# A two-layer stick-breaking/RWKV-7 and gMLP trunk on one core: hidden tiles 2048 bytes apart, query/key weights in groups of four, elementwise steps moved from VectorE to ScalarE and GpSimd

## The chip, the cores and the metric

The kernel runs on one core of a Trainium2 chip. The metric is the device time of one execution in microseconds (us), taken as the median of several runs. "Before" is the kernel as it stood, "after" the one with the change.

## The reference, cut to what matters

The input is 256 positions of 2048 float32 values. There are two layers. Layer 0 mixes with 16 stick-breaking attention heads and 16 RWKV-7 heads, layer 1 with a gated unit; each is followed by a squared-ReLU MLP of 8192 hidden columns.

```python
for layer in range(DEPTH):                       # DEPTH = 2
    h = rms_norm(x, norm_mix[layer])
    mix = even_mixer(h, ...) if layer % 2 == 0 else odd_mixer(h, ...)
    x = x + mix
    h = rms_norm(x, norm_ffn[layer])
    x = x + jnp.square(jax.nn.relu(h @ ffn_w1[layer])) @ ffn_w2[layer]
return rms_norm(x, norm_final)

def rwkv7_time_mix(zb, mu, ...):                 # 16 heads of 64, the second half of even_mixer
    zs = zb + (prev(zb) - zb) * mu               # token shift
    r, k, v, xw, xa, xg = split(zs)
    decay, a, g = ...                            # small projections of xw, xa, xg
    kk = k * k_k; kk = kk / norm(kk)             # per head
    k_mod = k * (1.0 + (a - 1.0) * k_a)
    # per step: S = S * w + (S @ -kk) (kk * a)^T + v k_mod^T ; y = S @ r
    y = (y - mean) * rsqrt(var + LNX_EPS) * lnx_w + lnx_b
    bonus = sum(r * k_mod * r_k) * v
    return (y + bonus) * g
```

## The kernel before, in words

Activations lie transposed: a tile of 128 rows holds 128 channels, and its 256 columns are the positions. Every operand of a large product is split into a high part (`hi`, in the type fp32r) and the rest (`lo`), and a product is hi·hi + hi·lo + lo·hi. A hidden tile `h` therefore has 512 columns, 256 high and 256 low, which are 2048 bytes in each partition.

Weights stream from HBM in groups of `KG` = 2 row blocks by up to 512 columns: SP issues the DMAs, ACT casts `raw` to `hi` (L318), DVE subtracts for `lo` (L319), each with three buffers of 4096 bytes. Three loops consume them. `gemm_a` (L379, L382) loads a weight block as the stationary operand and streams an activation tile: 512 columns for `hi`, 256 for `lo`. `gemm_n` (L413 to L415) does the same in three passes of 256 columns. `gemm_b` (L434 to L436) loads the activation tile as the stationary operand and streams 512 weight columns.

Which loop meets which tiles matters below. In layer 0's MLP and in the odd layer's output projection, `gemm_a` streams `h` tiles (4 x 256 pairs of one L379 and one L382 matmul, and 256 such pairs). In layer 1's MLP, `gemm_b` loads `h` tiles for the second product (1440 matmuls of 512 columns, then `gemm_last`). The normalised input `xg` is one buffer whose tiles are 2048 bytes apart.

The pool `hid` hands out 16 buffers again and again. Through `htile` (L216) a tile is allocated with 32 columns too many, so that buffers are 2176 bytes apart, and starts 0 or 16 columns into its buffer. In the program's memory plan buffer number i starts at 66304 + 2176 i bytes: 66304 is a multiple of 256, so even-numbered buffers start at a multiple of 256 bytes and odd-numbered ones 128 bytes past one. The `hi` and `lo` weight buffers start at multiples of 256.

The mixer of layer 0 (`even_mixer`, `rwkv_pair`, `sb_pair`) runs eight pairs of RWKV heads and eight pairs of stick-breaking heads as generators, which are advanced one step after each piece of a weight product (`advance`), so that their small operations lie between the large matmuls. A recording layer then sets the order in which each engine issues. In `rwkv_pair`, in the order of a pair's life: the token shift on POOL and DVE (L821, L825); `kk` and its square (L882, L884); decay factors `E`, `Ei` (L893, L894); `km` (L898, L899); `Z` and `BK` on DVE and POOL (L920 to L923); `rk` for the bonus (L926); the products `pk` (L936); an inverse by levels (`plv`); the scan over four chunks of 64 positions, each `pa` (L1036), `xs` on ACT (L1037), `pa` again (L1043), `SV` on ACT and DVE (L1044, L1045), `pc` (L1049); then the group norm: `var` (L1071), `rsqrt` by three Newton steps on DVE (L262 to L267), `yn` on POOL (L1085) and its transposes `pyt` on PE (L1090).

The two lines that set how long the group norm may take, in calls of the generator:

```python
W_PK, W_RS, W_YN = 2, 8, 4
for _ in range(W_RS): yield      # between rsqrt and yn; W_YN of them between yn and pyt
```

Of the kernel before, what the change touches and what calls it, by code (L numbers as in the profile page):

```python
# [8 lines left out]
F32 = mybir.dt.float32  # L9
F32R = mybir.dt.float32r  # L10
I32 = mybir.dt.int32
AF = mybir.ActivationFunctionType
# [87 lines left out]
class Net:  # L100
# [28 lines left out]
    def load_consts(self):  # L129
        nc, a = self.nc, self.aps  # L130
        self.consts = self.cp.tile([P, NCONST], F32, name="consts")
        o1 = CONST_OFF["ident"][1]
        nc.scalar.dma_start(self.consts[:, 0:o1], a["consts"][:, 0:o1])
        self.cv = {n: self.consts[:, o:o + w] for n, (o, w) in CONST_OFF.items()}
        self.ident = self.cv["ident"]
        self.ones = self.cp.tile([P, P], F32, name="ones")
        nc.gpsimd.memset(self.ones, 1.0)
        self.xT = self.xp.tile([P, KT, T], F32, name="xT")
        prow = self.hp.tile([P, 544], F32, name="prow", tag="h")[:, 0:512]
        nc.gpsimd.memset(prow, 0.0)  # L140
        rows = [prow[:, i * P:(i + 1) * P] for i in range(NPROW)]

        def put(name, ap, n, w=P, q=nc.gpsimd):
            r0 = PARAM_ROWS[name]
            t, r = rows[r0 // P], r0 % P
            q.dma_start(t[r:r + n, 0:w], ap)

        put("norm_mix", a["norm_mix"].rearrange("l (k p) -> (l k) p", p=P), 32, q=nc.scalar)
        x = a["x"][0].rearrange("(b p) d -> p b d", p=P)
        self.xst = self.xp.tile([P, 2, 4, 6], F32, name="xst")  # L150
        self.xrow = []
        for g in range(4):
            self.xrow.append([])
            for b in range(2):
                t = self.hp.tile([P, 544], F32, name="xrow", tag="h")[:, 0:512]
                nc.sync.dma_start(t, x[:, b, g * 512:(g + 1) * 512])
                self.xrow[g].append(t)
        put("norm_ffn", a["norm_ffn"].rearrange("l (k p) -> (l k) p", p=P), 32)
        mu = a["even_mu"]
        put("even_mu", mu[0, 0:3328].rearrange("(k p) -> k p", p=P), 26)  # L160
        r = PARAM_ROWS["even_mu"] + 26
        nc.gpsimd.dma_start(rows[r // P][r % P:r % P + 1, 0:32], mu[0:1, 3328:3360])
        for n in ("w0", "a0", "k_k", "k_a", "lnx_w", "lnx_b"):
            put("even_" + n, a["even_" + n][0].rearrange("(k p) -> k p", p=P), 8)
        put("even_r_k", a["even_r_k"][0].rearrange("(k h) p -> k (h p)", h=2), 8)
        self.par = self.cp.tile([P, NPROWS], F32, name="par")
        self.prow = rows
# [45 lines left out]
        self.rrow = self.xp.tile([P, T], F32, name="rrow")  # L213
        nc.vector.tensor_copy(self.rrow, ps[:, 0:T])

    def htile(self, o):  # L216
        return self.hp.tile([P, 2 * T + 32], F32R, name="h")[:, o:o + 2 * T]

    def new_norm(self, name, layer):
        buf = self.xp.tile([P, KT * 2 * T + 32], F32R, name="xg")  # L220
        o = XG_START[name, layer]
# [35 lines left out]
        nc.vector.tensor_scalar(m, ps[:, 0:2], 1.0 / D, RMS_EPS, op0=ALU.mult, op1=ALU.add)  # L257
        return m

    def rsqrt(self, out, m, q):  # L260
        nc = self.nc
        nc.vector.tensor_scalar(out.bitcast(I32), m.bitcast(I32), 1, None, op0=ALU.logical_shift_right)  # L262
        nc.vector.tensor_scalar(out.bitcast(I32), out.bitcast(I32), -1, 0x5F3759DF, op0=ALU.mult, op1=ALU.add)
        for _ in range(3):
            nc.vector.tensor_tensor(q, out, out, op=ALU.mult)
            nc.vector.scalar_tensor_tensor(q, q, -0.5, m, op0=ALU.mult, op1=ALU.mult)
            nc.vector.scalar_tensor_tensor(out, q, 1.5, out, op0=ALU.add, op1=ALU.mult)  # L267
# [214 lines left out]
    def ffn(self, layer, last):  # L482
# [8 lines left out]
                self.to_tokens()  # L491

        for q in range(4):
            hs = [self.htile(0 if last else 16) for _ in range(KT)]
            for c in range(4):
                def evac(n, ps):
                    a = self.combine(ps)
# [105 lines left out]
    def odd_mixer(self):  # L603
        nc, a = self.nc, self.aps
        w_in = a["odd_w_in"][0]
        with self.tc.tile_pool(name="odd", bufs=1) as op:
# [44 lines left out]
                        yield  # L651
                        nc.vector.tensor_tensor(v, v, lnb[:, s], op=ALU.add)

            ys = [self.htile(0) for _ in range(KT)]
            two = lambda t: t.rearrange("p (b t) -> p b t", b=2)

            def mix(c, us):
# [34 lines left out]
    def even_mixer(self):  # L692
        nc, a = self.nc, self.aps
        w_in = a["even_w_in"][0]
        with self.tc.tile_pool(name="mix", bufs=1) as mp:
# [1 line left out]
            self.new_norm("norm_mix", 0)  # L697
            xg = self.xg
            opnd = lambda k: xg[:, k]
            ys = [self.htile(0) for _ in range(KT)]  # L700
            self.dup = mp.tile([P, 2, T], F32R, name="dup")
            self.fold = [(mp.tile([P, NCH, 2, C], F32, name=f"Td{i}"), mp.tile([P, NCH, 4, C], F32, name=f"RBT{i}"))
                         for i in range(2)]
# [77 lines left out]
            def sb(j):  # L781
# [8 lines left out]
                        nc.vector.tensor_tensor(o, z[:, ::-1], self.rrow[:, ::-1], op=ALU.mult)  # L790
                    qk[n] = o

                self.gemm_n(w_in, 0, [(j * P, P), (SBW + j * P, P)], [P] * 2, opnd, evac_qk)
                self.bg.append((self.sb_pair(j, qk[0], qk[1], vt, ys[j]), 3, j))

            for j in range(NPAIR):
# [25 lines left out]
        return s  # L822

    def shift_mix(self, s, z, mu, rows):
        self.nc.vector.scalar_tensor_tensor(s[0:rows], s[0:rows], mu[0:rows], z[0:rows, 1:T + 1], op0=ALU.mult, op1=ALU.add)  # L825

    def shift(self, z, mu, rows):
        s = self.shift_sub(z, rows)
# [3 lines left out]
    def rwkv_pair(self, j, rkv, y_out):  # L832
# [46 lines left out]
        mix = lambda n, s: self.shift_mix(s, rkv[n], self.pcol("even_mu", n * 8 + j), P)  # L879
        mix(1, k)  # L880
        kk = st("kk")
        nc.vector.tensor_scalar(kk, k, self.pcol("even_k_k", j), None, op0=ALU.mult)  # L882
        kk2 = st("kk2")
        nc.scalar.square(kk2, kk)  # L884
        yield
        cs = st("cs", NCH * W1)
        nc.vector.tensor_tensor_scan(cs, cv["reset"], sig, 0.0, op0=ALU.mult, op1=ALU.add)
# [7 lines left out]
        yield  # L895
        mix(0, r)
        km = st("km")
        nc.vector.tensor_scalar(km, ai, self.hka[:, j:j + 1], self.oka[:, j:j + 1], op0=ALU.mult, op1=ALU.add)  # L898
        nc.vector.tensor_tensor(km, km, k, op=ALU.mult)  # L899
        pb = self.bank("pn2")  # L900
        for c in range(NCH):
# [21 lines left out]
            nc.gpsimd.tensor_tensor(Z[g, h, :, 1 - h], E3[g, :, 1:W1], ch(r)[g], op=ALU.mult)  # L923
            yield
        rk = st("rk")
        nc.vector.scalar_tensor_tensor(rk, r, self.pcol("even_r_k", j), km, op0=ALU.mult, op1=ALU.mult)  # L926
        for _ in range(W_PK):
            yield
        A = self.tmp("A", bufs=2, tag="comb")
# [142 lines left out]
        yield  # L1072
        rs = mt("rs", NCH)
        rq = mt("rsq", NCH)
        self.rsqrt(rs, var, rq)
        for _ in range(W_RS):
            yield
        yn = st("yn")
# [105 lines left out]
```

## Time and profile before

| | before |
|---|---|
| median of 3 runs | 2323.26 us (2320.88 to 2326.68) |
| the profiled execution, own time | 2320.03 us |
| its span | 2318.3 us |
| PE busy | 2271.3 us, 98% |
| DVE busy | 1492.6 us, 64% |
| ACT busy | 1056.0 us, 46% |
| POOL busy | 367.0 us, 16% |
| DMA | 400.98 MB, mean 173 GB/s |
| chain that ended last, by engine | PE 85%, DVE 8%, DMA 2%, ACT 2%, issue 1%, POOL 1% |

The span is the profiled execution from its first to its last instruction; 1.7 us of its time lie around it. PE's row of busy tenths reads 7 in the first of 40 slices, 8 in the last and 9 in between. The mixer of layer 0 fills the first 475 us, its output projection the next 107; the MLP of layer 0 begins at 582 us, the odd layer at 1306, and the MLP of layer 1 at 1590.

### The profile page before, as it was taken

To read this page: it belongs to the slowest core of one execution; us is meant where nothing else is said; L and a number is where in the kernel's file an instruction comes from. 1 tells how busy PE (TensorE), PEld (TensorE's weight loads), DVE (VectorE), ACT (ScalarE), POOL (GpSimd) and SP (SyncE) were. 2 spreads that over 40 slices of the span, in tenths; PEclk is the share of its full clock that TensorE was granted. 3 is DMA by queue.
4 is the path that set the end of the run, shared out by engine and by line. 5 is a ranking of instruction groups with operands and counts; after the bars stand their busy time and mean duration, and the time that the engine had idled before them with its cause. 6 is when DMAs were issued, how large, how long until landed. Compare 5 with 4: busy or idle time off the path is not lost.

```text
span 2318.3 us, 40151 instructions
## 1 busy us (share of the span) xinstructions
PE 2271.3 (98%) x15818; PEld 1988.1 (86%) x15818; DVE 1492.6 (64%) x2324; ACT 1056.0 (46%) x1571; POOL 367.0 (16%) x498
## 2 busy tenths in 40 slices
PE   7999999999999999999999999999999999999998
PEld 7788888889888888888888889988888888888887
DVE  6778888867655565565567758677555654654655
ACT  5435554444444444454444443444444443543443
POOL 2223333324004103103202202022000000000000
PEclk9999999999999999999999999999999999999999
DMA  6434434365665665665665565565656656666664
GB/s 183 140 108 107 128 105 107 103 196 179 206 186 187 191 186 186 191 187 187 189 188 175 185 191 165 172 200 164 198 189 188 188 190 192 187 189 190 189 189 138
DMA packets 276254, 400.98 MB, mean 173 GB/s; under 512 B 15852, under 2 KB 107489, under 8 KB 275681
## 3 DMA queue, kind: packets, MB, share of 16 engines
q1 hardware_dynamic: 273360, 393.03, 55.9%
q10 hardware_dynamic: 2384, 5.33, 0.6%
q8 instruction: 124, 2.03, 0.4%
q14 instruction: 66, 0.53, 0.1%
q0 software_dynamic: 320, 0.06, 0.0%
HBM read 396.26 MB, written 2.10 MB: 172 GB/s over the span
## 4 chain that ended last, share of the span: by engine, by line
PE 85%; DVE 8%; DMA 2%; ACT 2%; issue 1%; POOL 1%; SPq 0%; DVEq 0%; ACTq 0%; POOLq 0%
PE gm L379 13%; PE g L379 12%; PE gl L379 7%; PE gm L382 6%; PE g L382 6%; PE g L413 4%; PE gl L382 4%; PE g L414 4%; PE g L415 4%; PE g L434 3%; PE g L435 3%; PE g L436 3%; DVE lo L319 3%; PE gm L436 2%; PE gm L434 2%; PE gm L435 2%
## 5 line engine op out<-in xcount | busy, mean ns | idle before, releaser
L319 DVE TENSOR_TENSOR lo<-rawd,hi 128x1024 fp32r<-128x1024 f32 x600 | 749.4, 1250 | 625.2 <-ACT hi L318 620.0
L318 ACT CAST hi<-rawd 128x1024 fp32r<-128x1024 f32 x600 | 629.9, 1050 | 818.1 <-PE gm L379 254.8
L379 PE MATMUL g<-xg,hi 128*128 128x512 f32 x768 | 278.5, 394 | 0.0
L379 PE MATMUL gm<-xg,hi 128*128 128x512 f32 x768 | 272.8, 394 | 0.0
L413 PE MATMUL g<-xg,hi 128*128 128x256 f32 (+1 forms) x848 | 257.3, 305 | 2.6 <-ACT hi L318 2.6
L415 PE MATMUL g<-xg,lo 128*128 128x256 f32 (+1 forms) x848 | 240.2, 284 | 4.1 <-DVE lo L319 4.1
L414 PE MATMUL g<-xg,hi 128*128 128x256 f32 (+1 forms) x848 | 240.8, 284 | 0.6 <-DVE xg L232 0.6
L318 ACT CAST hi<-raw 128x768 fp32r<-128x768 f32 (+3 forms) x187 | 151.5, 812 | 195.4 <-PE g L414 99.8
L319 DVE TENSOR_TENSOR lo<-raw,hi 128x768 fp32r<-128x768 f32 (+3 forms) x187 | 180.4, 968 | 79.8 <-ACT hi L318 76.8
L382 PE MATMUL g<-xg,lo 128*128 128x256 f32 x768 | 207.9, 281 | 0.0
L382 PE MATMUL gm<-xg,lo 128*128 128x256 f32 x768 | 207.6, 280 | 0.0
L379 PE MATMUL gm<-h,hi 128*128 128x512 f32 x528 | 189.0, 396 | 0.0
L379 PE MATMUL gl<-xg,hi 128*128 128x512 f32 x512 | 184.7, 395 | 0.4 <-ACT hi L318 0.4
L379 PE MATMUL g<-h,hi 128*128 128x512 f32 x496 | 180.9, 397 | 0.0
L413 PEld LDWEIGHTS g<-xg,hi 128*128 128x128 f32 (+1 forms) x848 | 159.7, 189 | 9.7 <-ACT hi L318 3.0
L379 PEld LDWEIGHTS g<-xg,hi 128*128 128x128 f32 x768 | 142.2, 188 | 29.5
L379 PEld LDWEIGHTS gm<-xg,hi 128*128 128x128 f32 x768 | 142.1, 188 | 29.2
L415 PEld LDWEIGHTS g<-xg,lo 128*128 128x128 f32 (+1 forms) x848 | 159.7, 188 | 6.6 <-DVE lo L319 5.4
L414 PEld LDWEIGHTS g<-xg,hi 128*128 128x128 f32 (+1 forms) x848 | 160.3, 189 | 2.2 <-DVE xg L232 1.1
L382 PEld LDWEIGHTS gm<-xg,lo 128*128 128x128 f32 x768 | 144.0, 187 | 4.3
L382 PEld LDWEIGHTS g<-xg,lo 128*128 128x128 f32 x768 | 144.0, 188 | 4.2
L382 PE MATMUL gm<-h,lo 128*128 128x256 f32 x528 | 143.3, 281 | 0.0
(369 smaller groups left out, 4542.7 us busy)
## 6 DMA issues: line engine op xcount, KB each, us to landing
rawd<-ffn_w SPq DMA_DIRECT2D x509, 512.0 KB, 3.8
rawd<-odd_w_in SPq DMA_DIRECT2D x64, 512.0 KB, 4.2
raw<-even_w_in SPq DMA_DIRECT2D x128, 192.0 KB, 2.8
raw<-even_w_in SPq DMA_DIRECT2D x128, 128.0 KB, 2.3
raw<-even_w_out SPq DMA_DIRECT2D x32, 512.0 KB, 4.3
rawd<-odd_w_out SPq DMA_DIRECT2D x32, 512.0 KB, 4.2
raw<-even_w_in SPq DMA_DIRECT2D x16, 512.0 KB, 3.7
raw<-even_w_in SPq DMA_DIRECT2D x8, 288.0 KB, 3.3
```

The costliest lines, as they stand in the source:

```text
L318: nc.scalar.copy(hi[:, :, 0:width], raw[:, :, 0:width])
L319: nc.vector.tensor_tensor(lo[:, :, 0:width], raw[:, :, 0:width], hi[:, :, 0:width].bitcast(F32), op=ALU.subtract)
L379: nc.tensor.matmul(ps[n][0:wd], hi[:, kk, o:o + wd], x, start=first, stop=last)
L382: nc.tensor.matmul(ps[n][0:wd, T:2 * T], lo[:, kk, o:o + wd], x[:, 0:T], start=False, stop=False)
L413: nc.tensor.matmul(d, wh, x[:, 0:T], start=first, stop=False)
L414: nc.tensor.matmul(d, wh, x[:, T:2 * T], start=False, stop=False)
L415: nc.tensor.matmul(d, wl, x[:, 0:T], start=False, stop=last)
L434: nc.tensor.matmul(ps[b], xh, hi[:, kk], start=k == 0, stop=False)
L435: nc.tensor.matmul(ps[b], xh, lo[:, kk], start=False, stop=False)
L436: nc.tensor.matmul(ps[b], xl, hi[:, kk], start=False, stop=k == KT - 1)
```

## The change

`htile` is gone: `h`, `xrow` and `prow` tiles are allocated at their own 2048 bytes, so that every `h` tile starts at a multiple of 256 bytes. The query/key product takes its weights in groups of four row blocks instead of two, so each of its groups is one cast and one subtraction of 1024 columns in place of two of 512, with the same DMAs. In `shift_mix`, for `kk` and for `rk` a multiplication by a column goes to ACT, and so does the multiply-add of `km`; `shift_mix` and `rk` keep an addition or a multiplication on DVE. The square of `kk` is taken from `k`. The Newton steps of the group norm go from 9 operations of 128x4 on DVE to 12 on POOL.

```diff
-        prow = self.hp.tile([P, 544], F32, name="prow", tag="h")[:, 0:512]
+        prow = self.hp.tile([P, 512], F32, name="prow", tag="h")
...
-                t = self.hp.tile([P, 544], F32, name="xrow", tag="h")[:, 0:512]
+                t = self.hp.tile([P, 512], F32, name="xrow", tag="h")
...
-    def htile(self, o):
-        return self.hp.tile([P, 2 * T + 32], F32R, name="h")[:, o:o + 2 * T]
-
...
-    def rsqrt(self, out, m, q):
+    def rsqrt(self, out, m, q, pool=False):
...
         for _ in range(3):
+            if pool:
+                nc.gpsimd.tensor_tensor(q, out, out, op=ALU.mult)
+                nc.gpsimd.tensor_tensor(q, q, m, op=ALU.mult)
+                nc.gpsimd.tensor_scalar(q, q, -0.5, 1.5, op0=ALU.mult, op1=ALU.add)
+                nc.gpsimd.tensor_tensor(out, out, q, op=ALU.mult)
+                continue
             nc.vector.tensor_tensor(q, out, out, op=ALU.mult)
...
-            hs = [self.htile(0 if last else 16) for _ in range(KT)]
+            hs = [self.hp.tile([P, 2 * T], F32R, name="h") for _ in range(KT)]
...
-            ys = [self.htile(0) for _ in range(KT)]
+            ys = [self.hp.tile([P, 2 * T], F32R, name="h") for _ in range(KT)]
...
-                self.gemm_n(w_in, 0, [(j * P, P), (SBW + j * P, P)], [P] * 2, opnd, evac_qk)
+                self.gemm_n(w_in, 0, [(j * P, P), (SBW + j * P, P)], [P] * 2, opnd, evac_qk,
+                            tuple(range(NKG // 2)), kg_size=2 * KG)
...
-        self.nc.vector.scalar_tensor_tensor(s[0:rows], s[0:rows], mu[0:rows], z[0:rows, 1:T + 1], op0=ALU.mult, op1=ALU.add)
+        self.nc.scalar.activation(s[0:rows], s[0:rows], AF.Copy, scale=mu[0:rows])
+        self.nc.vector.tensor_tensor(s[0:rows], s[0:rows], z[0:rows, 1:T + 1], op=ALU.add)
...
-        nc.vector.tensor_scalar(kk, k, self.pcol("even_k_k", j), None, op0=ALU.mult)
+        nc.scalar.activation(kk, k, AF.Copy, scale=self.pcol("even_k_k", j))
         kk2 = st("kk2")
-        nc.scalar.square(kk2, kk)
+        nc.scalar.activation(kk2, k, AF.Square, scale=self.pcol("even_k_k", j))
...
-        nc.vector.tensor_scalar(km, ai, self.hka[:, j:j + 1], self.oka[:, j:j + 1], op0=ALU.mult, op1=ALU.add)
+        nc.scalar.activation(km, ai, AF.Identity, bias=self.oka[:, j:j + 1], scale=self.hka[:, j:j + 1])
...
-        nc.vector.scalar_tensor_tensor(rk, r, self.pcol("even_r_k", j), km, op0=ALU.mult, op1=ALU.mult)
+        nc.scalar.activation(rk, r, AF.Copy, scale=self.pcol("even_r_k", j))
+        nc.vector.tensor_tensor(rk, rk, km, op=ALU.mult)
...
-        self.rsqrt(rs, var, rq)
+        self.rsqrt(rs, var, rq, pool=True)
```

The order of issue changes with it. **POOL, where the second pair's `Z` and `BK` meet the first pair's `yn`.** Before:

```order
L923 TENSOR_TENSOR Z<-E,zs 64x4x64 x2
L922 TENSOR_TENSOR BK<-km,Ei 64x4x64 x2
L1085 TENSOR_TENSOR yn<-yc,rs 64x2x64 x4
L963 MEMSET SV 64x64 x2
L871 MEMSET sig 128x4
```

The change, from the second of the three Newton steps (L263 to L266 there) on:

```order
L263 TENSOR_TENSOR rsq<-rs 128x4
L264 TENSOR_TENSOR rsq<-rsq,var 128x4
L265 TENSOR_SCALAR rsq<-rsq 128x4
L928 TENSOR_TENSOR Z<-E,zs 64x4x64
L266 TENSOR_TENSOR rs<-rs,rsq 128x4
L928 TENSOR_TENSOR Z<-E,zs 64x4x64
L263 TENSOR_TENSOR rsq<-rs 128x4
L264 TENSOR_TENSOR rsq<-rsq,var 128x4
L265 TENSOR_SCALAR rsq<-rsq 128x4
L266 TENSOR_TENSOR rs<-rs,rsq 128x4
L1091 TENSOR_TENSOR yn<-yc,rs 64x2x64
L927 TENSOR_TENSOR BK<-km,Ei 64x4x64 x2
```

All twelve Newton operations and one `yn` now stand ahead of `BK`; on PE `pk`, which needs `Z` and `BK`, keeps its place among the large matmuls there.

**ACT, at the start of the fifth pair, from `ai` to the second chunk's `xs` of the pair before it.** Before:

```order
L874 ACTIVATE ai<-pa,ha_480 128x256
L876 COPY gate<-pw 128x256
L884 ACTIVATE kk_3835<-kk 128x256
L318 CAST hi<-raw 128x2x256
L852 CAST up<-lw 64x128
L893 ACT_TABLE_LOAD
L893 ACTIVATE Ei<-cs 128x256
L894 ACTIVATE E<-cs 128x260
L1037 COPY xs<-pa_3745 128x128
```

The change:

```order
L879 ACTIVATE ai<-pa,ha_480 128x256
L881 COPY gate<-pw 128x256
L887 ACTIVATE kk<-zs,par 128x256
L889 ACTIVATE kk_3826<-zs,par 128x256
L829 ACTIVATE zs<-zs,par 128x256
L857 CAST up<-lw 64x128 x2
L321 CAST hi<-raw 128x1024
L898 ACT_TABLE_LOAD
L898 ACTIVATE Ei<-cs 128x256
L899 ACTIVATE E<-cs 128x260
L903 ACTIVATE km<-ai,oka,hka 128x256
L1043 COPY xs<-pa_3733 128x128
```

`kk`, one token shift, `km` and a second `up` have come in ahead of `xs`, and the cast is twice as wide.

**PE, the third chunk of the same scan**, where L413 to L415 (L416 to L418 in the change) are large matmuls. Before, twelve of them stand between `pa` (L1043) and `pc`, of which the last four are shown:

```order
L414 MATMUL g<-xg,hi 128x256
L415 MATMUL g<-xg,lo 128x256
L1049 MATMUL pc_3746<-SV,RBT_143 128x64 x2
L413 MATMUL g<-xg,hi 128x256
L414 MATMUL g<-xg,hi 128x256
L415 MATMUL g<-xg,lo 128x256
```

The change:

```order
L1042 MATMUL pa_3733<-SV,Z 128x64
L417 MATMUL g<-xg,hi 128x256
L418 MATMUL g<-xg,lo 128x256
L416 MATMUL g<-xg,hi 128x256
L417 MATMUL g<-xg,hi 128x256
L1049 MATMUL pa_3733<-xs,Td_142 128x128
L418 MATMUL g<-xg,lo 128x256
L942 MATMUL pk<-Z,BK 128x128 x2
L1055 MATMUL pc_3734<-SV,RBT_143 128x64
L942 MATMUL pk<-Z,BK 128x128
L1055 MATMUL pc_3734<-SV,RBT_143 128x64
L942 MATMUL pk<-Z,BK 128x128 x5
```

One large matmul and two of `pk` now stand between `pa` and `pc`.

## Rows read from the trace of the kernel before

**Rows 1.** Busy time by engine in the mixer: stretch, width, PE, PEld, DVE, ACT, POOL.

```profile
100.00:510.00 410.00, 395.94 (x4847) 354.65 (x4846) 326.84 (x768) 196.51 (x400) 133.40 (x238) 1.00 0.43 118
```

**Rows 2.** What PE waited for in that stretch: total, times, longest.

```profile
PE pyt L1090 <- POOL yn L1085: 1.2, 1, 1.2
```

**Rows 3.** Groups of instructions, PE, whole span, large matmuls with `h`: busy, mean ns.

```profile
L379 PE MATMUL gm<-h,hi 128*128 128x512 f32 x528 | 189.0, 396 | 0.0
...
L382 PE MATMUL gm<-h,lo 128*128 128x256 f32 x528 | 143.3, 281 | 0.0
...
L434 PE MATMUL g<-hi,h 128*128 128x512 f32 x192 | 75.4, 393 | 0.0
```

**Rows 4.** The same, 1345 to 1390 us: `gemm_b` with `xg`.

```profile
L434 PE MATMUL gm<-hi,xg 128*128 128x512 f32 x40 | 15.6, 389 | 0.0
```

**Rows 5.** The same, 1688 to 1694.6 us: `gemm_b` with `h` in odd-numbered buffers.

```profile
L435 PE MATMUL gl<-lo,h 128*128 128x512 f32 x10 | 4.0, 395 | 0.0
```

**Rows 6.** The same, 1697.4 to 1703 us: `gemm_b` with `h` in even-numbered buffers.

```profile
L435 PE MATMUL gl<-lo,h 128*128 128x512 f32 x9 | 3.5, 389 | 0.0
```

**Rows 7.** Timeline of PE, odd output projection, even-numbered buffers: start, duration in us.

```profile
1539.82 0.40 PE L379 MATMUL g<-h,hi 128*128 128x512 f32 x1
...
1540.88 0.40 PE L379 MATMUL g<-h,hi 128*128 128x512 f32 x1
```

**Rows 8.** The same, an earlier stretch with even-numbered buffers.

```profile
1515.63 0.39 PE L379 MATMUL g<-h,hi 128*128 128x512 f32 x1
...
1517.01 0.39 PE L379 MATMUL gm<-h,hi 128*128 128x512 f32 x1
```

**Rows 9.** Groups of instructions, DVE, 0 to 575 us.

```profile
L319 DVE TENSOR_TENSOR lo<-raw,hi 128x1024 fp32r<-128x1024 f32 x47 | 59.9, 1279 | 31.6 <-ACT hi L318 30.0 <-PE g L414 0.8 <-PE g L415 0.5
L319 DVE TENSOR_TENSOR lo<-raw,hi 128x512 fp32r<-128x512 f32 x64 | 47.6, 745 | 17.8 <-ACT hi L318 17.0 <-PE pa L1043 0.3
L825 DVE SCALAR_TENSOR_TENSOR zs<-zs,par,z 128x256 f32<-128x256 f32 x26 | 18.1, 718 | 1.7 <-POOL zs L821 0.9
...
L265 DVE TENSOR_TENSOR rsq<-rs 128x4 f32<-128x4 f32 x24 | 5.4, 224 | 0.2
...
L267 DVE SCALAR_TENSOR_TENSOR rs<-rsq,rs 128x4 f32<-128x4 f32 x24 | 4.5, 189 | 0.1
...
L882 DVE TENSOR_SCALAR kk<-zs,par 128x256 f32<-128x256 f32 x8 | 3.4, 428 | 0.1
```

**Rows 10.** Groups of instructions, ACT, 0 to 575 us.

```profile
L884 ACT ACTIVATE kk<-kk 128x256 f32<-128x256 f32 x8 | 3.4, 420 | 2.5 <-DVE kk L882 2.5
```

**Rows 11.** Single lines on POOL: times, shortest/median/longest ns, first and last start.

```profile
L1158 POOL COPY rawd<-xT x5: 174/174/377, 586.0 to 586.7; 128x1 f32<-128x1 f32 x5
L1041 POOL TENSOR_SCALAR Sq<-SV,qe x32: 437/586/1483, 101.2 to 479.6; 64x64 f32<-64x64 f32 x32
L1085 POOL TENSOR_TENSOR yn<-yc,rs x32: 392/680/1314, 129.6 to 499.0; 64x128 f32<-64x128 f32 x32
```

**Rows 12.** Timeline, end of the first pair: POOL and PE.

```profile
123.59 2.03 POOL L923 TENSOR_TENSOR Z<-E,zs 64x256 f32<-64x256 f32 x2 [5.17 <-ACT E L894]
125.69 1.93 POOL L922 TENSOR_TENSOR BK<-km,Ei 64x256 f32<-64x256 f32 x2
128.25 1.64 PE L936 MATMUL pk<-Z,BK 64*128 64x128 f32 x14 [1.14 <-DVE BK L921]
```

**Rows 13.** Timeline, end of the fourth pair: POOL and PE.

```profile
305.44 3.09 POOL L1085 TENSOR_TENSOR yn<-yc,rs 64x128 f32<-64x128 f32 x4 [6.20 <-DVE rs L267]
309.91 0.27 PE L1090 MATMUL pyt<-consts,yn 128*128 128x128 f32 x1
```

**Rows 14.** Timeline, end of the last pair: DVE, POOL and PE.

```profile
493.13 0.16 DVE L265 TENSOR_TENSOR rsq<-rs 128x4 f32<-128x4 f32 x1
496.98 3.34 POOL L1085 TENSOR_TENSOR yn<-yc,rs 64x128 f32<-64x128 f32 x4 [0.96 <-DVE rs L267]
500.38 0.44 PE L1090 MATMUL pyt<-consts,yn 128*128 128x128 f32 x2 [1.16 <-POOL yn L1085]
```

More of the change, by code (lines that the diff above doesn't have):

```diff
@@ L699, in even_mixer @@
             opnd = lambda k: xg[:, k]
-            ys = [self.htile(0) for _ in range(KT)]
+            ys = [self.hp.tile([P, 2 * T], F32R, name="h") for _ in range(KT)]
             self.dup = mp.tile([P, 2, T], F32R, name="dup")
```

## The prediction

> **What bounds the kernel now.** I read the busy times of a stretch first, then what PE waits for in it, then the groups of instructions by line, and last the timelines of the places that the change touches. TensorE's row of busy tenths is full from the end of the mixer to the last layer, so there only the pace of the matmuls themselves counts. In the mixer from 100 to 510 us PE is busy for 395.94 of 410 us at a granted clock of 1.00, which is the 2.4 GHz level; DVE is busy for 326.84, ACT for 196.51 and POOL for 133.40 [rows 1]. So PE bounds the mixer too, and a step there can win at most the 410 - 395.94 = 14.06 us that PE idles, 1.2 of them on `yn` of the group norm [rows 2]. DVE has 83 us to spare, ACT and POOL over 200.
>
> The change thus has two sides. New tile addresses can alter the pace of matmuls anywhere. Everything else moves small operations that lie beside PE, and counts only where PE is made to wait longer or shorter.
>
> **1. Tiles 2048 bytes apart, `gemm_b` (layer 1's second product).** Its 512-column matmuls with an `h` tile as stationary operand take 393 ns in one group of 192 [rows 3]; six such groups and the rest make 1440. Sorted by buffer, the even-numbered ones, which start at a multiple of 256 bytes, give 389 ns [rows 6], as `xg` does [rows 4]; the odd-numbered, 128 bytes past one, give 395 [rows 5]. After the change all start at a multiple of 256. If half the tiles were odd the mean now would be 392, and the group says 393: 3 to 4 ns times 1440 are 4.3 to 5.8 us. I take **-5.3 us** (3.7 ns). Bounds: -5.8, and 0 if the durations, whose ends are modelled, don't show in the pace.
>
> Here stands a rule against the change. The Trainium skill, "TensorE: Matmul & The Clock Gate", section "Step-by-step: what each phase is for", says that the weights for the next matmul are read through a port of their own and take no read bandwidth from the running one. By it no address could matter, and this term would be 0. 389 against 395 in the same loop speak against that [rows 5, 6], so the sum goes by the rows; that nothing changes is rival 4.
>
> **2. The same tiles in `gemm_a`** (layer 0's second product and the odd projection, 1024 + 256 = 1280 pairs of a 512- and a 256-column matmul). Now `hi` takes 396 ns and `lo` 281 on average [rows 3]. In tiles that already start at a multiple of 256 two rhythms occur: three pairs in 1540.88 - 1539.82 = 1.06 us, 353 ns a pair [rows 7], and after a pause four pairs in 1517.01 - 1515.63 = 1.38 us, 345 ns [rows 8]. The first holds longer, and 1280 pairs run without a pause: I take **0**. Bounds: 0 and, at 6 ns a pair, -7.7 us (rival 2).
>
> **3. DVE relieved in the mixer.** Newton's three lines take 5.4 us, 4.5, and about 5.0 for the one between them; `kk` takes 3.4, and `km`'s multiply-add about as much, being the same operation of the same shape; 64 subtractions of 745 ns become 32 of 1279, 47.6 - 40.9 = 6.7 us less; the 26 shifts now cost 718 ns each, and an addition in their place costs between 428, the tile's price with one operand, and 718, so 0 to 7.5 us less [rows 9]. In all 28 to 36 of DVE's 327 us go. DVE isn't the bound, so that is worth only what PE waits on it: at most the idle 14.06 less the 1.2 on `yn`, 12.9 us. Most of these waits end on chains through DVE, ACT and POOL, and two thirds of a chain's links are not made shorter here; I take a third, **-4.3 us**. Bounds: -12.9 (rival 3), and 0.
>
> **4. ACT loaded.** An operation of 128x256 takes 420 ns there [rows 10]. ACT gets 27 shifts, `kk`, `km` and `rk` for eight pairs, some 51 x 0.42 = 21 us, and saves 32 casts; it is less than half busy, so its time is hidden, but not its order. In front of a second chunk's `xs` now stand up to four such operations, up to 1.7 us. PE's new order covers that: the second `pa` moved back behind more large matmuls. The price is in the third chunk, where one large matmul (0.12 us, a third of a pair [rows 7]) and two `pk` (1.64 / 14 = 0.117 us each [rows 12]) stand between `pa` and `pc`, in place of twelve large ones: 0.35 us of cover. `SV` needs an ACT and a DVE operation in that time: at most 0.84 us at two 420s, at least one, 0.42. I take 0.75, as the tiles are smaller, so 0.4 us of waiting in each of six pairs that have this order, **+2.4 us**. Bounds: 0 and 6 x (0.84 - 0.35) = +2.9, or +5 if DVE is late as well. A gain is excluded, as PE's order is nowhere looser for it.
>
> **5. Newton on POOL.** Twelve operations of 128x4 replace nine on DVE. The trace has none of this shape on POOL. Bounds for one: 0.174 us (128x1, the shortest copy) and 0.68, the median of `yn`, which is 392 ns at its shortest and 1314 at its longest; a 64x64 `tensor_scalar` takes 437 at its shortest [rows 11]. By size the row nearest is the first. I take 0.30 with the gap behind it, an estimate, so 3.5 us for the twelve; bounds 2.1 and 12 x (0.70 + 0.06) = 9.1. DVE's steps now take 496.98 - 493.13 = 3.85 us [rows 14], so alone POOL is no slower. What counts is its queue:
> - First pair: `Z` and `BK` of the second pair are ahead of the `pk` on PE. `BK` ends at 125.69 + 1.93 = 127.62 and `pk` starts at 128.25, having waited 1.14 us already [rows 12]. Twelve operations (3.5) and one `yn` (0.4) now stand before `BK`: it ends at about 131.5, `pk` waits until then, **+3.3 us**. In the second pair some 0.4 us of the same is left.
> - Middle pairs: `yn` ends at 305.44 + 3.09 = 308.53 and PE wants it at 309.91 [rows 13], 1.38 us of slack. POOL's 3.5 us are no more than DVE's 3.85: **0**. Of five such pairs none waits while an operation with its gap stays below (3.85 + 1.38) / 12 = 0.44 us.
> - Last pair: PE waits 1.16 us for `yn` already [rows 14], so each delay counts. Two mask operations of POOL come in between (0.68 each, taken as `yn`'s median) and DVE works beside; three of the twelve at 0.70 instead of 0.30: 3.5 + 1.36 + 1.2 - 3.85 = **+2.2 us**.
>
> Together +5.9, with bounds -1.2 (`yn`'s wait gone, no delay to `BK`) and about +28.
>
> **Sum:** -5.3 - 4.3 + 2.4 + 5.9 = -1.3 us. The profiled execution took 2320.03 us, the median is 3.2 above it: 2318.7 on the one scale, **2321.9** on the other.
>
> **The rivals.**
> *1, slower: POOL's small operations are blocked as `yn` is.* The same `yn` takes 392 ns or 1314 [rows 11], so something stretches POOL's operations by up to 0.9 us while DVE is 80% busy. Above 0.44 us an operation, five middle pairs begin to wait. At 0.60 they lose 5 x (7.2 - 5.23) = 9.9, the first pair 7.2 - 3.5 = 3.7 more, the last about 1: +15, 2337. At 0.76: 5 x 3.9 + 5.6 + 3 = +28, 2350. Against it: 128x4 is a thirtieth of `yn`'s columns, and DVE is relieved. Chance 0.22, middle 2337. Beside it: the Trainium skill, "SBUF — State Buffer", section "Who interferes with whom", says that one pair of ports is shared by the two engines and held by one of them for a whole instruction, the other blocking; by that rule, any of the twelve can be held up by a long instruction of DVE, and the spread of `yn` agrees.
> *2, faster: the shorter rhythm holds* in `gemm_a` with all tiles at multiples of 256 (for it [rows 8]; against it, [rows 7] from the same kind of tile): 2321.9 - 7.7 = 2314.2. Chance 0.14.
> *3, faster: DVE was behind nearly all of PE's idling in the mixer*; 8.6 us more go: 2313.3. For it, DVE is the busiest engine beside PE; against it, `pyt` waits on POOL [rows 2]. Chance 0.10.
> *4, the placement does nothing:* pitch is set by something else than a tile's start, 2321.9 + 5.3 = 2327.2. For it, durations are modelled; against it, `xg` and the even buffers agree to the nanosecond [rows 4, 6]. Chance 0.12.
> The forecast keeps 0.42.
>
> **How the numbers follow.** About 0.3%, 7 us, is what a measurement of this kernel can tell from no change: faster is below 2316.3, slower above 2330.2. The forecast's own range, with term 3 at 0 or at half of 12.9 and `pk`'s delay halved or doubled, is about 2317 to 2329; rival 4 lies within it. Faster: rivals 2 and 3 nearly whole, 0.23 with a rest for overlaps elsewhere. Slower: rival 1 and 0.02 of the forecast, 0.24. Same: 0.53. Down to 2309 (rivals 2 and 3 in part together) and up to 2340 (rival 1 past its middle) a fifth is left out.
>
> **What would show it.** Step 1: `gemm_b` with `h` at a mean of 389 ns in every stretch of layer 1. Step 2: 396 and 281 unchanged; near 390, rival 2. Step 3: DVE at about 295 us in the mixer. Step 4: six waits of `pc` near 0.4 us. Step 5: Newton on POOL in about 3.5 us, `pk` of the second pair waiting some 4 us, and `pyt` waiting in the last pair alone. Wrong would be: `pyt` waiting in most pairs (rival 1), or 393 ns still in layer 1 (rival 4).

## The result: 0.5% slower, and the profile after

The changed kernel takes 2333.76 us (median of 6 runs, 2332.95 to 2335.20), the kernel before 2324.97 in the same comparison. Its six runs hold a slow one of 3141 us, which the ratio leaves out; the median of the other five is 2323.26. The ratio is 1.0051, 95% interval 1.0041 to 1.0061, so **11.8 us are lost** (10.5 by the two medians). The profiled execution has a span of 2332.5 us, against 2318.3.

The stretch of the mixer in the profile after, which answers to [rows 1] (columns: stretch, width, PE, PEld, DVE, ACT, POOL, granted clock, DMA share, GB/s):

```profile
100.00:510.00 410.00, 390.65 (x4744) 349.87 (x4743) 297.52 (x630) 201.69 (x397) 159.52 (x313) 0.98 0.42 112
```

DVE is relieved by 29 us, as worked out, and POOL has 26 more. Yet PE idles for 19.4 us where it idled for 14.06, at a granted clock of 0.98 instead of 1.00. What PE waited for in the whole span, for [rows 2] (total, times, longest):

```profile
PE pk L942 <- POOL BK L927: 10.3, 2, 5.2
PE pyt L1096 <- POOL yn L1091: 5.2, 3, 3.5
...
PE pc L1055 <- DVE SV L1051: 3.8, 6, 0.7
```

Two new waits of 5.2 us stand out. PE doesn't wait for `xs` here. Groups of instructions of the whole span and of 1600 to 2300 us, for [rows 3] and [rows 5]:

```profile
L382 PE MATMUL gm<-h,hi 128*128 128x512 f32 x528 | 189.0, 397 | 0.0
...
L385 PE MATMUL gm<-h,lo 128*128 128x256 f32 x528 | 143.0, 280 | 0.0
...
L437 PE MATMUL g<-hi,h 128*128 128x512 f32 x192 | 74.7, 389 | 0.0
```

`gemm_b` with `h` is at 389 ns everywhere, `gemm_a` unchanged.

**Where the time went.** Both kernels issue the same number of large matmuls, so the start of each, counted from the first, can be set against the other kernel's. The last column does the same for the change with its Newton steps back on DVE, a run that is described below:

| us before | place | late by, us | without Newton on POOL |
|---|---|---|---|
| 117.5 | first pair's group norm still to come | 4.5 | 2.7 |
| 155.2 | behind the second pair's `pk` | 9.7 | 3.5 |
| 184.7 | | 9.8 | 3.6 |
| 200.1 | behind the third pair's `pk` | 15.0 | 3.05 |
| 489.4 | before the last group norm | 21.1 | 8.6 |
| 505.2 | behind it | 23.1 | 8.6 |
| 579.4 | end of the output projection | 21.2 | 6.7 |
| 1592.8 | layer 1's MLP begins | 21.05 | 8.2 |
| 2308.4 | its last large matmul | 14.5 | 1.65 |

Layer 1's MLP wins 6.6 us. From one start to the next, its 1440 matmuls of `gemm_b` with `h` take 226.7 ns where they took 230.4, which makes 5.4 us, the first term; 1.5 come from the first product's `gemm_a` with `xg` (1024 pairs), which no term had. All the loss lies in the mixer: 4.5 us before the first Newton step, two jumps of 5.2 at `pk`, 2.0 at the last pair, and 6 us spread over the middle pairs; 1.9 come back at the end. The difference of the two columns is Newton's part. From 117.5 us on it grows by 4.5 at the second pair's `pk`, 5.7 at the third's, 0.6 in the middle pairs and 2.0 at the last: 12.8 in all. The 6 us of the middle pairs are in both columns, so they aren't Newton's.

The first jump, in the timeline of DVE, POOL and PE (start, duration in us):

```profile
126.96 1.22 DVE L322 TENSOR_TENSOR lo<-raw,hi 128x1024 fp32r<-128x1024 f32 x1
126.98 1.26 POOL L263 TENSOR_TENSOR rsq<-rs 128x4 f32<-128x4 f32 x1 [1.10 <-DVE rs L260]
...
131.48 1.55 POOL L928 TENSOR_TENSOR Z<-E,zs 64x256 f32<-64x256 f32 x1
...
133.94 0.20 POOL L266 TENSOR_TENSOR rs<-rs,rsq 128x4 f32<-128x4 f32 x1
134.22 0.40 POOL L1091 TENSOR_TENSOR yn<-yc,rs 64x128 f32<-64x128 f32 x1
134.69 1.51 POOL L927 TENSOR_TENSOR BK<-km,Ei 64x256 f32<-64x256 f32 x2
135.46 2.87 PE L942 MATMUL pk<-Z,BK 64*128 64x128 f32 x16 [5.16 <-POOL BK L927]
...
138.85 0.63 PE L438 MATMUL g<-lo,xg 128*128 128x512 f32 x1
139.28 0.63 PE L439 MATMUL g<-hi,xg 128*128 128x512 f32 x1
...
142.88 0.39 PE L439 MATMUL g<-hi,xg 128*128 128x512 f32 x1
143.11 0.39 PE L437 MATMUL g<-hi,xg 128*128 128x512 f32 x1
```

`BK` stands behind the whole chain of Newton steps and one `yn`, and starts at 134.69 where it started at 125.69 [rows 12]; of these 9 us 4.5 had been lost before. Behind the wait PE starts a 512-column matmul every 0.43 us instead of every 0.23: it runs at the level of 1.2 GHz. The stretches of the two long waits, cut where the pace changes:

```profile
136.00:142.60 6.60, 6.60 (x27) 5.51 (x26) 3.16 (x7) 1.38 (x2) 1.68 (x7) 0.50 0.00 0
142.60:150.00 7.40, 7.40 (x95) 5.46 (x93) 5.63 (x13) 3.16 (x8) 0.00 (x0) 1.00 0.25 66
...
201.00:207.00 6.00, 6.00 (x31) 5.48 (x32) 3.06 (x6) 0.60 (x1) 0.99 (x4) 0.50 0.00 1
```

A granted clock of 0.50 over 6.6 and 6.0 us of busy PE is work for 3.3 and 3.0 us at full clock: each long wait costs some 3 us more behind its end. (Before, the clock fell after the shorter wait of [rows 12] too, to 0.93 and 0.90 over 20 us, 1.7 us in all.)

The first Newton operation above took 1.26 us, where the shortest of the same line took 0.20: it started with a 1.22 us subtraction on DVE and ended with it. The Trainium skill, "SBUF — State Buffer", section "Who interferes with whom", has an instruction of DVE with two SBUF inputs contend with an instruction of POOL that reads SBUF, over a read port that the two share; these two rows agree.

**The middle pairs, slower without waiting.** The same 3729 matmuls, between the same two large ones, in the kernel before and in the change (columns as above):

```profile
200.10:489.40 289.30, 280.07 (x3729) 255.52 (x3727) 235.71 (x566) 144.02 (x296) 97.46 (x171) 1.00 0.43 116
214.70:510.20 295.50, 286.49 (x3729) 258.73 (x3727) 225.43 (x483) 151.82 (x298) 122.47 (x232) 1.00 0.42 113
```

The granted clock is 1.00 in both and PE idles no longer, 9.0 us in place of 9.2; it is PE's busy time that has grown, by 6.4. Half of that is in `pk`. Before, the sixteen `pk` of a pair are issued in a row; in the change `pc` stands between them, which has the form 128*128 where `pk` has 64*128. The fifth pair, before and after:

```profile
285.36 1.16 PE L936 MATMUL pk<-Z,BK 64*128 64x128 f32 x16
286.45 0.38 PE L413 MATMUL g<-xg,hi 128*128 128x256 f32 x1
...
301.70 0.49 PE L942 MATMUL pk<-Z,BK 64*128 64x128 f32 x4
302.12 0.43 PE L1055 MATMUL pc<-SV,RBT 128*128 128x64 f32 x2
302.49 0.49 PE L942 MATMUL pk<-Z,BK 64*128 64x128 f32 x2
302.90 0.43 PE L1055 MATMUL pc<-SV,RBT 128*128 128x64 f32 x2
303.27 0.93 PE L942 MATMUL pk<-Z,BK 64*128 64x128 f32 x10
304.13 0.39 PE L416 MATMUL g<-xg,hi 128*128 128x256 f32 x1
```

Sixteen in a row hold PE for 286.45 - 285.36 = 1.09 us until the next matmul starts; in three pieces they hold it for 0.42 + 0.41 + 0.86 = 1.69. Over the 80 `pk` of this stretch that is 3.1 us. The run without Newton on POOL has it too; with tiles and groups of four alone the 80 take 0.2 us more than before, with the four moves to ACT alone 2.0, so it comes with these. The other 3 us are spread over many groups and were not traced.

### The profile page after: what moved, and what is told of

The parts are those of the page before. It is cut to its first block, busy times and chain, and to the rows that moved or that the text cites. A ratio compares the mean times of both kernels' runs of the same rounds, so it can differ in the third digit from the quotient of the medians.

```text
span 2332.5 us, 40091 instructions
## 1 busy us (share of the span) xinstructions
PE 2276.6 (98%) x15818; PEld 1996.7 (86%) x15818; DVE 1472.2 (63%) x2204; ACT 1072.9 (46%) x1590; POOL 404.1 (17%) x594
## 4 chain that ended last, share of the span: by engine, by line
PE 87%; DVE 6%; POOL 2%; ACT 2%; issue 1%; DMA 1%; DVEq 0%; SPq 0%; ACTq 0%; POOLq 0%
PE gm L382 13%; PE g L382 12%; PE gl L382 7%; PE gm L385 6%; PE g L385 6%; PE g L416 4%; PE g L418 4%; PE g L417 4%; PE gl L385 4%; PE g L437 3%; PE g L438 3%; PE g L439 3%; DVE lo L322 2%; PE gm L439 2%; PE gm L437 2%; PE gm L438 2%
## 5 line engine op out<-in xcount | busy, mean ns | idle before, releaser
L416 PE MATMUL g<-xg,hi 128*128 128x256 f32 (+1 forms) x848 | 259.2, 307 | 3.0 <-ACT hi L321 2.6
L418 PE MATMUL g<-xg,lo 128*128 128x256 f32 (+1 forms) x848 | 241.8, 286 | 4.3 <-DVE lo L322 4.3
L321 ACT CAST hi<-raw 128x1024 fp32r<-128x1024 f32 (+2 forms) x155 | 145.5, 941 | 196.1 <-PE g L417 123.4
L322 DVE TENSOR_TENSOR lo<-raw,hi 128x1024 fp32r<-128x1024 f32 (+2 forms) x155 | 176.7, 1144 | 77.2 <-ACT hi L321 71.1
L382 PE MATMUL gl<-xg,hi 128*128 128x512 f32 x512 | 184.7, 394 | 0.7 <-ACT hi L321 0.7
L416 PEld LDWEIGHTS g<-xg,hi 128*128 128x128 f32 (+1 forms) x848 | 161.0, 190 | 11.1 <-ACT hi L321 3.1
L418 PEld LDWEIGHTS g<-xg,lo 128*128 128x128 f32 (+1 forms) x848 | 161.1, 190 | 5.8 <-DVE lo L322 5.3
```

Of the source, the lines that this page charges most:

```text
L321: nc.scalar.copy(hi[:, :, 0:width], raw[:, :, 0:width])
L322: nc.vector.tensor_tensor(lo[:, :, 0:width], raw[:, :, 0:width], hi[:, :, 0:width].bitcast(F32), op=ALU.subtract)
L382: nc.tensor.matmul(ps[n][0:wd], hi[:, kk, o:o + wd], x, start=first, stop=last)
L416: nc.tensor.matmul(d, wh, x[:, 0:T], start=first, stop=False)
L418: nc.tensor.matmul(d, wl, x[:, 0:T], start=False, stop=last)
```

## The experiments

Times below are the ratio to the kernel before, and that times 2322 us. Each comparison had at least five runs of the kernel; an interval is some 2.3 us to either side, wider for the shortest series. The ratio of two medians can differ from the ratio given by up to 2 us.

### Only the tiles

```diff
-            hs = [self.htile(0 if last else 16) for _ in range(KT)]
+            hs = [self.hp.tile([P, 2 * T], F32R, name="h") for _ in range(KT)]
```

with the same for `ys`, `xrow` and `prow`.

> The kernel before with the tiles of h, xrow and prow 2048 bytes apart, and nothing else. In the changed kernel the same large matmul of layer 1's MLP starts 21.05 us late at 1590 us and the last one 14.5 us late, so 6.5 us are won there. If this is the placement's doing, the kernel is 6 to 7 us faster than before, gemm_b with h reads 389 ns, and gemm_a with h stays at 396 and 281. Rival: the gain in layer 1 comes from another timing of the stream after a later mixer; then this kernel is within 2 us of before.

Measured: 0.9971 (0.9961 to 0.9982), **-6.7 us**. Groups of instructions:

```profile
L431 PE MATMUL g<-hi,h 128*128 128x512 f32 x192 | 74.7, 389 | 0.0
...
L376 PE MATMUL gm<-h,hi 128*128 128x512 f32 x528 | 189.2, 397 | 0.0
```

The gain is the placement's: 5.4 us in `gemm_b` by the starts, which come every 226.7 ns in all profiled versions with the new tiles and every 230.4 in all without. Here too 1.5 us more come from layer 1's `gemm_a` with `xg`, whose `hi` matmuls start every 230.8 ns in place of 232.0; why was not looked into.

### Only Newton on POOL, and in which pairs

```diff
-        self.rsqrt(rs, var, rq)
+        self.rsqrt(rs, var, rq, pool=True)
```

> The kernel before with only the Newton steps on POOL. Theory: the change's loss is mostly this. Ten or more Newton operations of 0.4 to 0.5 us stand ahead of the second and third pairs' BK on POOL; pk on PE waits 3.5 to 5 us for each, and behind each wait the granted clock falls to 0.50 for some microseconds, 1.5 to 2.5 us more each. Expected 9 to 14 us slower than before, two waits of pk on BK of 3.5 to 5 us each. Rival: most of the loss comes with ACT's added operations or the wide groups, and Newton alone costs no more than the 3 to 6 us forecast.

Measured: 1.0042 (1.0030 to 1.0055), **+9.8 us**.

```diff
+        self.rsqrt(rs, var, rq, pool=2 <= j <= 6)
```

> The kernel before with the Newton steps on POOL in the third to the seventh pair only; the first, second and last keep them on DVE. If Newton's price is that of a queue (Z and BK of the next pair behind it, and yn at the end of the mixer), these five pairs cost little: 0 to 3 us slower than before. If it is the price of an operation, every pair's yn comes late and it is 5 to 7 us slower, five eighths of the 9.5 us of all eight.

Measured: 0.9994 (0.9986 to 1.0003): no difference.

```diff
+        self.rsqrt(rs, var, rq, pool=not 2 <= j <= 6)
```

> The kernel before with the Newton steps on POOL in the first, second and last pair only, the complement of the run of the five middle pairs, which cost nothing. If the queue in front of BK and the end of the mixer make the price, all of Newton's loss is here: 8 to 12 us slower than before, with two waits of pk on BK of 3 to 5 us and one of pyt on yn. If the loss needs all eight, 3 to 6 us slower.

Measured: 1.0047 (1.0033 to 1.0061), **+10.9 us**. Three pairs of eight carry all of it. What PE waits for there, 100 to 560 us:

```profile
PE pk L942 <- POOL BK L928: 8.0, 4, 4.1
PE pyt L1096 <- POOL yn L1091: 3.6, 1, 3.6
```

and with the five middle pairs instead:

```profile
PE pk L942 <- DVE BK L927: 2.9, 3, 1.5
...
PE pyt L1096 <- POOL yn L1091: 1.2, 1, 1.2
```

The second answer is that of the kernel before, to 0.1 us. Yet an operation on POOL isn't shorter there. The four operations of a step in the middle pairs, groups on POOL:

```profile
L268 POOL TENSOR_SCALAR rsq<-rsq 128x4 f32<-128x4 f32 x15 | 8.1, 541 | 1.4
L266 POOL TENSOR_TENSOR rsq<-rs 128x4 f32<-128x4 f32 x15 | 6.5, 434 | 6.9 <-DVE rs L263 6.0
L267 POOL TENSOR_TENSOR rsq<-rsq,var 128x4 f32<-128x4 f32 x15 | 6.0, 397 | 1.0
L269 POOL TENSOR_TENSOR rs<-rs,rsq 128x4 f32<-128x4 f32 x15 | 5.9, 395 | 1.2
```

26.5 us over 60 operations are 0.44 each, against 12.8 over 36, 0.36, in the three pairs of the other run:

```profile
L269 POOL TENSOR_TENSOR rs<-rs,rsq 128x4 f32<-128x4 f32 x9 | 3.8, 420 | 0.7
L266 POOL TENSOR_TENSOR rsq<-rs 128x4 f32<-128x4 f32 x9 | 3.3, 371 | 10.1 <-DVE rs L263 9.8
L268 POOL TENSOR_SCALAR rsq<-rsq 128x4 f32<-128x4 f32 x9 | 3.0, 329 | 0.5
L267 POOL TENSOR_TENSOR rsq<-rsq,var 128x4 f32<-128x4 f32 x9 | 2.7, 295 | 0.7
```

The slower operations cost nothing, the faster ones 10.9 us. The price is that of the place in the queue.

### The change without Newton on POOL

```diff
-        self.rsqrt(rs, var, rq, pool=True)
+        self.rsqrt(rs, var, rq)
```

> The changed kernel with the Newton steps back on DVE, all else kept. If Newton's steps in front of BK are the main loss, and cost more here than alone because other delays add to them (alone they cost 9.5 us), it is 10 to 14 us faster than the changed kernel, 2320 to 2324 us, and pk no longer waits on POOL. Rival: the parts simply add, and it is 2324 us or more, by as much as Newton alone had cost.

Measured: 0.9996 (0.9987 to 1.0005), 2322.01 us: 12.8 us faster than the change, by the two ratios. The rest of the change thus gives back in the mixer what the tiles win. Its mixer:

```profile
100.00:510.00 410.00, 396.48 (x4800) 352.63 (x4799) 317.69 (x721) 207.31 (x409) 134.66 (x237) 1.00 0.42 115
```

DVE has 9 us less than in [rows 1], and PE idles for 13.5 us instead of 14.06: the relief buys next to nothing. What this run loses lies in the middle pairs, 5.5 us from 200 to 489 us in the table above, at full clock, with `pk` in pieces.

### The moves to ACT, and one by one

All four (`shift_mix`, `kk` with its square, `km`, `rk`) on the kernel before:

```diff
+        self.nc.scalar.activation(s[0:rows], s[0:rows], AF.Copy, scale=mu[0:rows])
+        nc.scalar.activation(kk, k, AF.Copy, scale=self.pcol("even_k_k", j))
+        nc.scalar.activation(km, ai, AF.Identity, bias=self.oka[:, j:j + 1], scale=self.hka[:, j:j + 1])
+        nc.scalar.activation(rk, r, AF.Copy, scale=self.pcol("even_r_k", j))
```

> The kernel before with only shift, kk, km and rk scaled on ACT. In the changed kernel 4.5 us are lost before 90 us, where no Newton step has run yet. If ACT's operations cost them, this kernel is 3 to 8 us slower than before, with waits of pc on SV of 0.5 us each and a late ptk or ptv at 75 us. Rival: DVE is relieved and it is 0 to 4 us faster.

Measured: 1.0027 (1.0017 to 1.0037), **+6.3 us**. What PE waits for, and the longest of these waits with the pace behind it:

```profile
PE pa L1045 <- ACT xs L1039: 4.1, 3, 1.7
```

```profile
345.18 0.83 ACT L318 CAST hi<-raw 128x768 fp32r<-128x768 f32 x1 [4.87 <-DMA raw<-even_w_in]
345.92 0.26 ACT L1039 COPY xs<-pa 128x128 f32<-128x128 f32 x1
346.23 0.49 PE L1045 MATMUL pa<-xs,Td 128*128 128x128 f32 x2 [1.68 <-ACT xs L1039]
...
347.50 0.42 PE L415 MATMUL g<-xg,lo 128*128 128x256 f32 x1
347.72 0.41 PE L413 MATMUL g<-xg,hi 128*128 128x256 f32 x1
347.93 0.41 PE L414 MATMUL g<-xg,hi 128*128 128x256 f32 x1
```

Directly ahead of this `xs` on ACT stands a weight cast, as in the kernel before. Here it waits 4.87 us for its weights, and with it `xs` and PE, which afterwards starts a 256-column matmul every 0.21 us, where 0.12 is usual. The other two waits for `xs` also come directly behind such casts, before which ACT sat idle for 2.9 and 3.9 us. So ACT was not busy with the moved operations when `xs` was late; why its casts wait longer was not looked into. Set against the kernel before as in the table above, this run loses 7.2 us from 200 to 489 us. With tiles and groups of four alone, the same stretch is 1.4 us shorter than before. The waits of `pc` on `SV` that were expected don't show: there is one, of 0.3 us.

One by one, each line of the diff above alone (`kk` with its square):

> The kernel before with only the token shift scaled on ACT. The four moves to ACT cost 6.5 us together. If the shift carries them (27 operations on three engines in a row, and a new wait of DVE and of the next pair on ACT's queue), this is 4 to 7 us slower than before; if kk, km and rk carry them (they stand in front of xs), this is within 2 us.

> The kernel before with only km's multiply-add on ACT. The shift alone cost 0 to 2 us of the 6.5 that the four moves cost together, so kk, km and rk hold the rest. km stands in the chain that ends in BK and pk, and on ACT it comes behind the exponentials and in front of the other pair's xs. If it carries the loss, 3 to 6 us slower than before; if the loss lies in kk and rk, within 2 us.

> The kernel before with only kk, its square and rk scaled on ACT. If km carries the loss of the moves to ACT, this is within 2 us of before or up to 2 us faster; if the number of operations on ACT is what counts, it is 3 to 5 us slower.

> The kernel before with only kk and its square scaled on ACT. kk and rk together cost 4.1 us, with longer waits of ptk and ptv on RBT. If kk carries that, 3 to 5 us slower than before; if rk does, within 2 us.

> The kernel before with only rk scaled on ACT and multiplied on DVE. rk lies between Z and pk, in front of RBT, and now needs both engines. If it carries the 4.1 us of kk and rk together, 3 to 5 us slower than before; if kk does, within 2 us.

| alone | ratio, interval | us |
|---|---|---|
| shift | 1.0001 (0.9992 to 1.0009) | +0.2 |
| `km` | 0.9990 (0.9981 to 1.0000) | -2.3 |
| `kk` and `rk` | 1.0017 (1.0008 to 1.0026) | +3.9 |
| `kk` | 1.0010 (1.0001 to 1.0019) | +2.3 |
| `rk` | 1.0006 (0.9998 to 1.0015) | +1.4 |

No single one has the 6.3 us. `kk` and `rk` each alone add up to what the two cost together, 3.7 against 3.9; but shift, `km`, `kk` and `rk` add to 1.6. The difference of 4.7 us is about what intervals of 2.3 us on each of five ratios leave, so it does not prove that they act on each other. The wait of `pa` on `xs` of 1.7 us is that of the run with all four: with `kk` and `rk` alone the longest is 0.5 us. Which others make `xs` later was not tried.

### The groups of four, and the best version

```diff
-                self.gemm_n(w_in, 0, [(j * P, P), (SBW + j * P, P)], [P] * 2, opnd, evac_qk)
+                self.gemm_n(w_in, 0, [(j * P, P), (SBW + j * P, P)], [P] * 2, opnd, evac_qk,
+                            tuple(range(NKG // 2)), kg_size=2 * KG)
```

> The kernel before with only the query and key weights in groups of four row blocks. If the relief of DVE counts (6.7 us of 327 in the mixer) it is 0 to 2 us faster than before; if the wider casts and subtractions stand in the way of the small operations on ACT and DVE it is 1 to 4 us slower. The theory that Newton's steps are the main loss expects within 3 us of before.

Measured: 0.9994 (0.9985 to 1.0003): no difference that can be told.

The same edit and the tiles together:

> The kernel before with the tiles 2048 bytes apart and the query and key weights in groups of four, and nothing else. The two alone measured -7.3 and -1.6 us (the second not clear of nothing). If they add, 8 to 9 us faster than before, 2314 us; if the wide groups only shift where the clock falls, no faster than the tiles alone, 2315 to 2317.

Measured: 0.9956 (0.9942 to 0.9969), 2314.23 us, **-10.2 us** (8.2 by the medians), faster than both kernels. With Newton on POOL in the five middle pairs as well:

> The tiles and the groups of four as in the run of these two, and the Newton steps on POOL in the third to the seventh pair. That run measured 8.2 us faster than before, Newton in the five middle pairs 1.1 us faster (not clear of nothing). If the relief of DVE in the middle pairs counts, 2312 to 2314 us; if the waits there are ended by something else, 2314 to 2316, the same as without it.

Measured: 0.9963 (0.9951 to 0.9976), 2313.58 us: no further gain. And with `km` on ACT on top:

> Tiles, groups of four and Newton on POOL in the five middle pairs, and km's multiply-add on ACT: the parts that cost nothing alone or win. km alone measured 2.5 us faster than before. If that adds, 2310 to 2312 us; if it does not, 2313 to 2315.

Measured: 0.9980 (0.9971 to 0.9989), 2317.29 us. `km`'s gain alone, itself at the edge of its interval, does not add; the version is 3.7 us slower than without it by the medians, with intervals that still overlap.

## Why the prediction was wrong

Forecast was -1.3 us, measured +11.8. The step that failed most is the queue on POOL in front of `BK`: for the second pair's group norm it was put at 0.4 us of waiting and measured 3.5 with 3 more at half clock, and the half clock had no term anywhere. Beside it the relief of DVE was counted as 4.3 us and bought nothing clear of the noise, and the premise that a small operation "counts only where PE is made to wait longer or shorter" left out the 6 us of the middle pairs, where PE doesn't wait longer. Term by term:

1. **Tiles in `gemm_b`: right.** -5.3 forecast, -5.4 measured by the starts, 3.7 ns each over 1440 matmuls. Layer 1 as a whole wins 6.6 within the change and the tiles alone 6.7; the rest of that is the 1.5 us of `gemm_a` with `xg`. The rule that I set against it (the Trainium skill, "TensorE: Matmul & The Clock Gate", section "Step-by-step: what each phase is for": weights come through a port of their own and cost the running matmul no bandwidth), read as leaving no room for an effect of the address, would have had no gain at all. The measurement decides: a start 128 bytes off costs time in this loop. Rival 4 falls.
2. **Tiles in `gemm_a`: right**, 0. The shorter rhythm of rival 2 did not hold: 397 and 280 ns, and from the end of layer 0's projection to the start of layer 1's MLP the change stays late by 21 us, to 0.2.
3. **DVE's relief: wrong.** "I take a third, -4.3 us" was a choice with no row behind it, and no run shows a gain clear of its interval: the groups of four measure nothing alone, and Newton taken off DVE in five pairs measures nothing. In the middle pairs of the change (the stretch of 289.3 us above) PE's waits on DVE's tiles did fall, from 8.5 to 6.4 us, but waits on POOL took 1.6 of that back. Rival 3 falls too. The likely reason, that these waits end on chains in which DVE is one link of several, was not tested.
4. **ACT: the wait right, the order's other price left out.** `pc` waits on `SV` 3.8 us in six places, before 1.6 in five: +2.2, where 2.4 was forecast. "PE's new order covers that" held as well: neither the change nor the run without Newton has a wait for `xs`. But all four moves cost 6.3 us alone, and 9 (7.8 by the medians) lie between the tiles with groups of four (0.9956) and the change without Newton (0.9996). By the starts of the large matmuls these two runs part in the middle pairs, 6.9 us from 200 to 489 us. The forecast saw that PE's order puts two `pk` between `pa` and `pc`, and priced the wait of `pc` alone; the `pk` in pieces take some 3 us more there. The rest of the 6.9 stays open.
5. **Newton on POOL: right place, half the size.** 5.9 forecast, 9.8 alone, 12.8 within the change. The chain of twelve, put at 3.5 us, took 5.6 to 7.3 in the change, with what POOL does between them.
   - *First pair*: `pk` waits 5.16 instead of 1.14, +4.0, where 3.3 was forecast.
   - *Second pair*: "some 0.4 us of the same is left" was the worst step. Here all twelve operations and all four `yn` got ahead of `BK`, more than in the first pair, and it waits 5.17 us where two waits of `pk` there had 1.7. In the timeline:

```profile
197.97 0.20 POOL L266 TENSOR_TENSOR rs<-rs,rsq 128x4 f32<-128x4 f32 x1
198.25 1.75 POOL L1091 TENSOR_TENSOR yn<-yc,rs 64x128 f32<-64x128 f32 x4
200.08 1.51 POOL L927 TENSOR_TENSOR BK<-km,Ei 64x256 f32<-64x256 f32 x2
...
200.85 2.87 PE L942 MATMUL pk<-Z,BK 64*128 64x128 f32 x16 [5.17 <-POOL BK L927]
```

   - *Last pair*: +2.2 forecast; the wait is 3.5 instead of 1.16, +2.3.
   - *The clock* had no term at all. Both waits of 5.2 us are followed by 6.0 to 6.6 us at half clock, about 3 us each.

Rival 1 named the right sign and, with 2337 in its middle, nearly the right time, but that was luck: its mechanism, five middle pairs that wait for `yn`, hardly happened. An operation with its gap did pass its threshold of 0.44 us: 10.2, 12.6, 9.7 and 7.7 us over four lines of 24 are 0.42 each, and a gap of 0.08 follows (of the groups on POOL, two lines):

```profile
L264 POOL TENSOR_TENSOR rsq<-rsq,var 128x4 f32<-128x4 f32 x24 | 12.6, 525 | 1.7
L263 POOL TENSOR_TENSOR rsq<-rs 128x4 f32<-128x4 f32 x24 | 10.2, 425 | 10.1 <-DVE rs L260 8.1 <-DVE rn L913 0.6
```

Yet in the change only two of the five wait, 0.8 us each, and in the run of the five alone none does. The slack isn't the reason: before, the five have 1.20, 1.38, 1.38, 1.20 and 3.21 us of it. But the four `yn` behind the steps were taken to last as long as before, and in the run of the five alone they last 0.6 to 1.8 us less in four of them. In the third pair `yn` starts there 3.3 us later and ends 1.5 later, 260.11 instead of 258.62.

The 4.5 us by which the change is late before any Newton step has run are mostly not its own. A fall of the clock at 46 us makes 1.6 of them. It also shows in the run of the five middle pairs, which differs from the kernel before in nothing up to there, so it belongs to the single execution and not to the change. A second fall, to 0.50 from 77.7 to 81.1 us, makes 1.7. The run without Newton, which issues the same instructions up to there, waits at the same place without it and is 2.7 us late. What is left, about 1 us, is in that run as well, and so is a new wait of 0.9 us of `ptk` on `RBT`. The profiled execution of before is 3 us under its median, and the profile of after loses 14.2 us where the medians' ratio gives 11.8.

## What to carry to other kernels

A small operation moved to an idle engine is priced by what queues behind it in that engine's order, at each place anew: count the instructions ahead of every tile that a busy engine waits for, in every pair and not in one. Allow, behind a wait of TensorE of some microseconds, for a stretch at half clock: here it cost 60% of the 5.2 us once more. Look also at the order in which the busy engine itself issues: the same sixteen matmuls took 1.09 us in a row and 1.69 in three pieces. And relief of an engine that was 80% busy was worth nothing here that a run could show; it needs a wait that is named and ends sooner by it.

## What the runs showed of the hardware

- The start of a stationary tile at a multiple of 256 bytes or 128 past one changes the pace of 512-column fp32r matmuls: 389 against 395 ns, 5.4 us over 1440 matmuls of which half were odd.
- An operation of 128x4 on POOL takes 0.20 us at its shortest and 0.42 on average beside a busy DVE in the change; the median of `yn` fell from 680 [rows 11] to 396 ns at the same time, with 29 us less on DVE:

```profile
L1091 POOL TENSOR_TENSOR yn<-yc,rs x32: 392/396/1019, 134.2 to 522.7; 64x128 f32<-64x128 f32 x32
```

- Behind a wait of PE of 5.2 us the granted clock stood at 0.50 for 6.0 to 6.6 us of work. Behind 1.7 us (`xs`) it fell as well. Behind the last pair's wait for `yn` of 3.5 to 3.6 us it fell to 0.50 in the run with only Newton on POOL (513 to 515 us) and in that with three pairs of it (514 to 516), and stayed at 1.00 in the change (523 to 540).
- Sixteen matmuls of the form 64*128 (`pk`) took 1.09 us in a row and 1.69 in three pieces with matmuls of the form 128*128 (`pc`) between them, at a granted clock of 1.00. Whether it is the change of form or any other matmul between them that costs this was not tried.
